# Output blocks of a hybrid encoder held as two 2 KB halves in place of one 4 KB row, right half first

## The chip, the cores and the metric

One NeuronCore of a Trainium2 chip runs the whole program. The metric is the device time of one execution in microseconds (us); where several runs are shown, the median counts. The engines are named as in the profile: PE (TensorE, matrix products), DVE (VectorE), ACT (ScalarE), POOL (GpSimd) and SP, whose queue issues every DMA of this kernel. PEld is the weight load of PE.

## The reference

Two independent inputs, a prompt of 512 positions and a sample of 1024, go through the same encoder layer with shared weights (d = 1024), all in float32.

```
h = RMSNorm(x);  z = h @ w_in
A = windowed attention on q, k, v          # 8 heads, 128-wide window, sinks
B = silu(LayerNorm(dwconv31(a * sigmoid(b))))
x = x + concat(A, B) @ w_out
u = dwconv3(RMSNorm(x) @ w_up)
x = x + (silu(u[:, :2816]) * u[:, 2816:]) @ w_down
return RMSNorm(x)                          # y * rsqrt(mean(y*y) + eps) * norm_final_g
```

The change lies in the last line, the final RMSNorm of the rows, and in the stores of its result: 12 blocks of 128 rows by 1024 columns (8 of the sample, 4 of the prompt).

## The kernel before

The products are made in float32 precision out of three products of a high and a low part (`whi*hi`, `whi*lo`, `wlo*hi`); each high part is an ACT cast, each low part a subtraction on DVE or POOL. The down-projection of the last stage is cut into seven block products (a Strassen-like scheme, `ORDER = (1, 2, 5, 6, 7, 4, 3)`), each over 11 pairs of 128 rows of `w_down` (`p` = 0 to 10). The sums of the products lie in `acc` ("u", "e", "o11", "o12"), to which `with_x` adds the residual.

Product 4 is the last but one. After it the sums `u` and `e` are complete, so six output blocks can be finished while PE works on product 3: `finish` is called for them between the groups of that product, at the steps listed in `done_at`. When product 3 has been made for four further blocks, DVE adds it to `o12` (line 952 of the helper `add`) and `finish` is called for them; for the last two blocks (tt = 2 and 3) the product is made block by block, the left half having been prepared by `left_first`. In this text the output blocks are numbered 1 to 12 in the order of these calls: 1 to 6 within product 3, 7 to 10 after it, 11 and 12 at the end.

`finish` does this for one block, whose halves of 512 columns are called left (n = 0, from `parts[0]`) and right (n = 1): ACT squares each half with an accumulated sum and writes the squares, which nobody reads, into the output buffer `o` (L1471; L1463 for the left half of blocks 11 and 12). POOL turns the two sums into the root factor with three instructions on 128x1 (L1472, L1473, L1474). The left half is scaled by ACT (L1479) and multiplied by `norm_final_g` on POOL (L1480); in blocks 11 and 12 ACT's scaling (L1482) is all, the vector having been multiplied in on DVE before (L1464). The right half is one DVE instruction (L1484). Each half is stored by one DMA of 256 KB on SP (L1485).

Buffers come from `Slots`, a list of 15 buffers "q" of 4096 bytes, 4 "c" of 4224 and 61 "h" of 2048 per partition. `tile` gives out the smallest kind that fits and, in it, the buffer that has been free for longest; a buffer goes back to the end of the list when the program's last reference to it is gone. A new tile in a used buffer waits for all that read or wrote the old one, a store among them. In the last stage the operand halves of product 3 are "h" buffers too: steps p = 4 to 10 are cast while the first blocks are finished, at most four steps (`LEAD`) ahead.

PE and SP run in the order of the program (`manual_schedule`). On ACT, DVE and POOL a planner sorts the instructions when the program is built, and each of these queues is then worked off strictly in that order, so an instruction that waits holds all behind it.

Of the kernel before, what the change touches and what calls it, by code (L numbers as in the profile page):

```python
# [12 lines left out]
AF = mybir.ActivationFunctionType  # L13
ALU = mybir.AluOpType

P = 128
D = 1024
KC = D // P
NT = 512
# [126 lines left out]
def tile_hybrid_encoder(ctx: ExitStack, tc: tile.TileContext, xs, rel_bias, norm_attn_g, w_in,  # L146
                        attn_sink, conv_dw_w, conv_dw_b, conv_ln_g, conv_ln_b, w_out, norm_ffn_g,
                        w_up, ffn_dw_w, ffn_dw_b, w_down, norm_final_g, onehot, outs):
    nc = tc.nc
# [7 lines left out]
    sb = Slots(big, dict(q=(15, 4096), c=(4, 4224), h=(61, 2048), d=(2, 2176), s=(32, 64)), "q", KEEP)  # L157
# [3 lines left out]
    def sm(n):  # L161
        return sb.tile([n])
# [786 lines left out]
    L, R = slice(0, NT), slice(NT, W2)  # L949
# [506 lines left out]
    fins = []  # L1456
    early = {}

    def left_first(tt):

        ss, o = early[tt] = sm(2), sb.tile([D])
        part = cut(o11, tt)
        nc.scalar.activation(o[:, L], part, AF.Square, accum_out=ss[:, 0:1])  # L1463
        nc.vector.tensor_tensor(part, part, fins[0][:, L], op=ALU.mult)  # L1464

    def finish(blk, parts, tail):
        ss, o = early.pop(blk) if tail else (sm(2), sb.tile([D]))
        rs = sm(2)
        for n in range(1 if tail else 0, 2):
            s = slice(n * NT, (n + 1) * NT)  # L1470
            nc.scalar.activation(o[:, s], parts[n], AF.Square, accum_out=ss[:, n:n + 1])  # L1471
        nc.gpsimd.tensor_scalar(rs[:, 0:1], ss[:, 0:1], 1.0 / D, EPS, op0=ALU.mult, op1=ALU.add)  # L1472
        nc.gpsimd.tensor_scalar(rs[:, 1:2], ss[:, 1:2], 1.0 / D, rs[:, 0:1], op0=ALU.mult, op1=ALU.add)  # L1473
        nc.gpsimd.tensor_tensor(rs[:, 1:2], rs[:, 1:2], nhalf[:], op=ALU.pow)  # L1474
        G, b = (GR[1], blk) if blk >= 0 else (GR[0], blk + 4)
        for n in range(2):
            s = slice(n * NT, (n + 1) * NT)
            if n == 0 and not tail:
                nc.scalar.activation(o[:, s], parts[n], AF.Identity, scale=rs[:, 1:2])  # L1479
                nc.gpsimd.tensor_tensor(o[:, s], o[:, s], fins[0][:, s], op=ALU.mult)  # L1480
            elif n == 0:
                nc.scalar.activation(o[:, s], parts[n], AF.Identity, scale=rs[:, 1:2])  # L1482
            else:
                nc.vector.scalar_tensor_tensor(o[:, s], parts[n], rs[:, 1:2], fins[0][:, s], op0=ALU.mult, op1=ALU.mult)  # L1484
            nc.sync.dma_start(G["o"][b * P:(b + 1) * P, s], o[:, s])  # L1485

    made = 0

# [109 lines left out]
    for p, w in [(0, 2), (1, 2), (0, 0), (1, 0)] + [(p, w) for p in range(2, NPAIR) for w in (2, 0)]:  # L1598
        last_group(p, w)
        if w == 0 and p in done_at:  # L1600
            tt = done_at[p]
            finish(4 + tt if tt < 4 else tt - 6, (cut(u, tt), cut(e, tt)), False)
    for tt in (4, 5, 0, 1):
        add(cut(o12, tt), zs[tt // 2][:, (tt % 2) * NT:(tt % 2 + 1) * NT], cut(o12, tt))
        finish(tt if tt < 4 else tt - 8, (cut(o11, tt), cut(o12, tt)), False)
    zs.clear()
    for tt in (2, 3):
        left_first(tt)
        z = wide()
        for p in range(NPAIR):  # L1610
            mm_down(z[:, L], 3, p, tt)
        add(cut(o12, tt), z[:, L], cut(o12, tt))
        finish(tt, (cut(o11, tt), cut(o12, tt)), True)
        del z
# [43 lines left out]
```

## Time and profile before

| | us |
|---|---|
| runs shown | 1562.33, 1561.49, 1563.84 |
| median | 1562.33 |
| span of the profiled execution | 1559.5 |
| median of the runs less that span | 2.8 |
| PE busy in the span | 1505.8 (97%) |
| DVE, ACT, POOL busy | 1126.9, 795.2, 709.7 |
| HBM read, written | 164.74 MB, 62.14 MB |

The span runs from the first to the last event of the profiled execution; the profile gives no other time of that execution, so the 2.8 us are what lies around the span, as far as it can be told. All times within the run below are microseconds from the start of the span. In a row of the timeline stand start, duration, engine, line and operation, then output and inputs by name and the count of instructions merged into the row; in brackets the idle time of that engine just before, and what ended it. A row of the waits reads "engine line waited for: total, times, longest".

### The profile page before, as it was taken

The page shows a single profiled execution, that of the slowest core. Times are in us where ns is not written, and L with a number is a line of the kernel's source. Part 1 is how long each engine was busy: PE and PEld are TensorE (multiplying, and loading weights), DVE is VectorE, ACT ScalarE, POOL GpSimd, SP SyncE. Part 2 cuts the span into 40 slices and gives each one's busy share as a digit, 9 for nine tenths or more (in the row PEclk, how much of TensorE's full clock was granted, in tenths as well). Part 3 has the DMA queues.
Part 4 walks back from the last instruction along what each step waited for, and adds up shares of the span by engine and source line. Part 5 has one row for each costly group of instructions (what it writes and reads, how often), then busy time and mean ns, then how long its engine had stood idle before and what let it go on. Part 6 is the DMA issues. An engine that isn't in the chain of part 4 may idle for free. (4 is left out here: it accounts for less than half of the span.)

```text
span 1559.5 us, 20112 instructions
## 1 busy us (share of the span) xinstructions
PE 1505.8 (97%) x6843; PEld 1228.9 (79%) x6843; DVE 1126.9 (72%) x1604; ACT 795.2 (51%) x1404; POOL 709.7 (46%) x566
## 2 busy tenths in 40 slices
PE   8998998899999999899999999999999999999997
PEld 6787787787888888777777888888888788888885
DVE  7999767858789785334868777777776845569883
ACT  4634654335787786623455445554545543444354
POOL 6652343226666775947434555555544000003355
PEclk9999999899999999999999999999999999999999
DMA  7582334447344346779332333333332582357644
GB/s 229 157 212 78 108 99 124 128 131 226 111 132 130 117 130 182 241 235 305 108 95 75 102 101 102 102 102 102 102 115 75 191 280 82 105 166 233 220 132 162
DMA packets 228780, 227.17 MB, mean 146 GB/s; under 512 B 13268, under 2 KB 168348, under 8 KB 228549
## 3 DMA queue, kind: packets, MB, share of 16 engines
q1 hardware_dynamic: 228677, 225.88, 45.6%
q8 instruction: 54, 0.88, 0.2%
q14 instruction: 49, 0.40, 0.1%
HBM read 164.74 MB, written 62.14 MB: 145 GB/s over the span
## 5 line engine op out<-in xcount | busy, mean ns | idle before, releaser
L193 POOL TENSOR_TENSOR q<-q,q 128x1024 fp32r<-128x1024 f32 x72 | 173.3, 2414 | 93.5 <-ACT q L192 36.7
L955 POOL TENSOR_TENSOR q<-q,q 128x512 fp32r<-128x512 f32 x101 | 140.7, 1398 | 163.8 <-ACT q L1065 151.5
L955 DVE TENSOR_TENSOR h<-h,h 128x512 fp32r<-128x512 f32 (+2 forms) x202 | 158.4, 817 | 66.2 <-ACT h L959 26.1
L1413 PE MATMUL w<-h,h 128*128 128x512 f32 x462 | 181.4, 393 | 0.5 <-DVE q L1200 0.5
L1414 PE MATMUL w<-h,h 128*128 128x512 f32 x462 | 181.5, 393 | 0.0
L1415 PE MATMUL w<-h,h 128*128 128x512 f32 x462 | 181.1, 392 | 0.0
L1079 PE MATMUL w<-h,q 128*128 128x512 f32 x448 | 176.4, 394 | 3.0 <-ACT w L1171 1.6
L1081 PE MATMUL w<-h,q 128*128 128x512 f32 x448 | 175.5, 392 | 1.0 <-POOL q L955 1.0
L1080 PE MATMUL w<-h,q 128*128 128x512 f32 x426 | 166.5, 391 | 0.0
L299 PE MATMUL u<-h,q 128*128 128x512 f32 x400 | 161.1, 403 | 5.0 <-DVE h L852 4.2
L300 PE MATMUL u<-h,q 128*128 128x512 f32 x400 | 158.9, 398 | 0.0
L302 PE MATMUL u<-h,q 128*128 128x512 f32 x384 | 152.2, 396 | 2.7 <-POOL q L193 2.7
L952 POOL TENSOR_TENSOR q<-q,q 128x1024 f32<-128x1024 f32 x12 | 33.1, 2769 | 238.1 <-DMA h<-gb 197.4
L354 DVE SCALAR_TENSOR_TENSOR c<-c,cvw,c 128x512 f32<-128x512 f32 x184 | 137.9, 750 | 2.9
L959 ACT CAST h<-h 128x512 fp32r<-128x512 f32 x120 | 71.8, 619 | 95.9 <-DVE h L955 42.5
L299 PE MATMUL b<-h,q 128*128 128x512 f32 x256 | 102.3, 400 | 2.7 <-DVE d L384 1.9
L1413 PEld LDWEIGHTS w<-h,h 128*128 128x128 f32 x462 | 86.8, 188 | 20.7 <-ACT h L959 0.9
L1415 PEld LDWEIGHTS w<-h,h 128*128 128x128 f32 x462 | 86.7, 188 | 19.7
L852 DVE SCALAR_TENSOR_TENSOR h<-u,fw,h 128x511 f32<-128x511 f32 x88 | 65.4, 744 | 50.8 <-ACT h L856 50.1
L1414 PEld LDWEIGHTS w<-h,h 128*128 128x128 f32 x462 | 86.8, 188 | 19.4
L1079 PEld LDWEIGHTS w<-h,q 128*128 128x128 f32 x448 | 84.2, 188 | 22.5 <-ACT w L1171 2.1
L302 PE MATMUL b<-h,q 128*128 128x512 f32 x256 | 101.3, 396 | 0.0
(417 smaller groups left out, 3680.3 us busy)
## 6 DMA issues: line engine op xcount, KB each, us to landing
q<-in_w_up SPq DMA_DIRECT2D x88, 512.0 KB
ga<-q SPq DMA_DIRECT2D x64, 256.0 KB
h<-ga SPq DMA_DIRECT2D x57, 256.0 KB
q<-in_w_in SPq DMA_DIRECT2D x28, 512.0 KB
h<-in_w_down SPq DMA_DIRECT2D x52, 256.0 KB
q<-in_x_sample SPq DMA_DIRECT2D x15, 512.0 KB
h<-qsd SPq DMA_DIRECT2D x24, 256.0 KB
x1d<-q SPq DMA_DIRECT2D x11, 512.0 KB
```

Source lines behind the costliest of these rows:

```text
L193: (nc.vector if dve else nc.gpsimd).tensor_tensor(lo[:], raw[:], hi[:].bitcast(F32), op=ALU.subtract)
L299: nc.tensor.matmul(out, whi[:, kc, :], hi[:], start=(kc == 0), stop=False)
L300: nc.tensor.matmul(out, whi[:, kc, :], lo[:], start=False, stop=False)
L302: nc.tensor.matmul(out, wlo[:, kc, :], hi[:], start=False, stop=(kc == KC - 1))
L354: nc.vector.scalar_tensor_tensor(acc[:], src(t), w(t), acc[:], op0=ALU.mult, op1=ALU.add)
L955: (eng or nc.vector).tensor_tensor(out, a, b, op=ALU.subtract)
L1079: nc.tensor.matmul(out, whi[:, s], hi[:], start=(start and c == 0), stop=False, **go)
L1080: nc.tensor.matmul(out, whi[:, s], lo[:], start=False, stop=False, **go)
L1081: nc.tensor.matmul(out, wlo[:, s], hi[:], start=False, stop=(stop and c == 3), **go)
L1413: nc.tensor.matmul(out, sh[:, c], th[:], start=(p == 0), stop=False)
L1414: nc.tensor.matmul(out, sh[:, c], tl[:], start=False, stop=False)
L1415: nc.tensor.matmul(out, sl[:, c], th[:], start=False, stop=(p == NPAIR - 1))
```

## The change

An output block is held in two "h" buffers of 2 KB, `o[0]` for the left half and `o[1]` for the right, in place of one "q" buffer of 4 KB. The loop that scales and stores takes the right half first, so its DVE instruction is issued, and its store queued on SP, ahead of the left half's. The number of instructions and of stores stays as it was, and the functions after the change are one line shorter, so that lines 1471 to 1485 become 1470 to 1484.

```diff
     def left_first(tt):
 
-        ss, o = early[tt] = sm(2), sb.tile([D])
+        ss, o = early[tt] = sm(2), [sb.tile([NT]) for _ in range(2)]
         part = cut(o11, tt)
-        nc.scalar.activation(o[:, L], part, AF.Square, accum_out=ss[:, 0:1])
+        nc.scalar.activation(o[0][:], part, AF.Square, accum_out=ss[:, 0:1])
         nc.vector.tensor_tensor(part, part, fins[0][:, L], op=ALU.mult)
 
     def finish(blk, parts, tail):
-        ss, o = early.pop(blk) if tail else (sm(2), sb.tile([D]))
+        ss, o = early.pop(blk) if tail else (sm(2), [sb.tile([NT]) for _ in range(2)])
         rs = sm(2)
         for n in range(1 if tail else 0, 2):
-            s = slice(n * NT, (n + 1) * NT)
-            nc.scalar.activation(o[:, s], parts[n], AF.Square, accum_out=ss[:, n:n + 1])
+            nc.scalar.activation(o[n][:], parts[n], AF.Square, accum_out=ss[:, n:n + 1])
...
-        for n in range(2):
+        for n in (1, 0):
             s = slice(n * NT, (n + 1) * NT)
             if n == 0 and not tail:
-                nc.scalar.activation(o[:, s], parts[n], AF.Identity, scale=rs[:, 1:2])
-                nc.gpsimd.tensor_tensor(o[:, s], o[:, s], fins[0][:, s], op=ALU.mult)
+                nc.scalar.activation(o[n][:], parts[n], AF.Identity, scale=rs[:, 1:2])
+                nc.gpsimd.tensor_tensor(o[n][:], o[n][:], fins[0][:, s], op=ALU.mult)
             elif n == 0:
-                nc.scalar.activation(o[:, s], parts[n], AF.Identity, scale=rs[:, 1:2])
+                nc.scalar.activation(o[n][:], parts[n], AF.Identity, scale=rs[:, 1:2])
             else:
-                nc.vector.scalar_tensor_tensor(o[:, s], parts[n], rs[:, 1:2], fins[0][:, s], op0=ALU.mult, op1=ALU.mult)
-            nc.sync.dma_start(G["o"][b * P:(b + 1) * P, s], o[:, s])
+                nc.vector.scalar_tensor_tensor(o[n][:], parts[n], rs[:, 1:2], fins[0][:, s], op0=ALU.mult, op1=ALU.mult)
+            nc.sync.dma_start(G["o"][b * P:(b + 1) * P, s], o[n][:])
```

The orders below differ from the place of product 3 on; before that nothing moves. A name such as `h20_2215` is buffer 20 of kind h, with a running number of the tile; `s` are sums and factors, `c1` is the vector `norm_final_g`, `w` are PE's banks.

The first place is ACT's queue where blocks 6 to 10 are squared and scaled. Before, all of it lies in three buffers:

```order
L1471 ACTIVATE q5_2201_13880,s12_2200_13879<-q12_1797_11993 128x512
L1471 ACTIVATE q7_2204_13894,s14_2203_13893<-q12_1797_11993 128x512
L1471 ACTIVATE q0_2207_13908,s16_2206_13907<-q2_1794_11963 128x512
L1471 ACTIVATE q5_2201_13880,s12_2200_13879<-q9_1962_12760 128x512
L1471 ACTIVATE q7_2204_13894,s14_2203_13893<-q9_1962_12760 128x512
L1471 ACTIVATE q0_2207_13908,s16_2206_13907<-q8_1959_12728 128x512
L1479 ACTIVATE q5_2201_13880<-q12_1797_11993,s13_2202_13881 128x512
L1479 ACTIVATE q7_2204_13894<-q12_1797_11993,s15_2205_13895 128x512
L1479 ACTIVATE q0_2207_13908<-q2_1794_11963,s17_2208_13909 128x512
L1471 ACTIVATE q5_2210_13922,s18_2209_13921<-q2_1794_11963 128x512
L1471 ACTIVATE q5_2210_13922,s18_2209_13921<-q8_1959_12728 128x512
```

The same place with the change:

```order
L1470 ACTIVATE h50_2204_13860,s10_2202_13858<-q3_1873_12348 128x512
L1470 ACTIVATE h39_2207_13886,s12_2206_13885<-q12_1797_11993 128x512
L1478 ACTIVATE h26_2203_13859<-q13_1716_11610,s11_2205_13861 128x512
L1470 ACTIVATE h50_2211_13901,s14_2210_13900<-q12_1797_11993 128x512
L1470 ACTIVATE h20_2208_13887,s12_2206_13885<-q9_1962_12760 128x512
L1470 ACTIVATE h26_2212_13902,s14_2210_13900<-q9_1962_12760 128x512
L1478 ACTIVATE h39_2207_13886<-q12_1797_11993,s13_2209_13888 128x512
L1478 ACTIVATE h50_2211_13901<-q12_1797_11993,s15_2213_13903 128x512
L1470 ACTIVATE h20_2215_13916,s16_2214_13915<-q2_1794_11963 128x512
L1470 ACTIVATE h39_2216_13917,s16_2214_13915<-q8_1959_12728 128x512
L1470 ACTIVATE h26_2219_13931,s18_2218_13930<-q2_1794_11963 128x512
L1470 ACTIVATE h50_2220_13932,s18_2218_13930<-q8_1959_12728 128x512
```

Before, blocks 7, 8 and 9 (tiles 2201, 2204, 2207) take turns in q5, q7, q0 and block 10 (2210) is back in q5, the buffer of block 7. Now blocks 8 (2211 and 2212) and 10 (2219 and 2220) share h26 and h50 with block 6, and blocks 7 and 9 share h20 and h39: a block's halves lie where the halves of the block two before lay, the left where the right one lay.

The second place is ACT's queue where blocks 1 to 3 are scaled and the last operands of product 3 are cast. Before:

```order
L959 CAST h12_2172_13710<-h42_2121_13465 128x512
L1471 ACTIVATE q7_2170_13698,s2_2169_13697<-q11_1875_12365 128x512
L959 CAST h27_2185_13767<-h26_2133_13526 128x512
L1471 ACTIVATE q5_2157_13641,s0_2156_13640<-q1_1719_11629 128x512
L1471 ACTIVATE q5_2157_13641,s0_2156_13640<-q11_1875_12365 128x512
L1471 ACTIVATE q7_2170_13698,s2_2169_13697<-q1_1719_11629 128x512
L959 CAST h42_2187_13771<-h20_2140_13546 128x512
L1479 ACTIVATE q0_2179_13735<-q6_1713_11592,s5_2180_13736 128x512
L1479 ACTIVATE q5_2157_13641<-q1_1719_11629,s1_2158_13642 128x512
L1479 ACTIVATE q7_2170_13698<-q1_1719_11629,s3_2171_13699 128x512
```

With the change:

```order
L1478 ACTIVATE h55_2181_13737<-q6_1713_11592,s5_2183_13739 128x512
L1478 ACTIVATE h46_2157_13641<-q1_1719_11629,s1_2159_13643 128x512
L1478 ACTIVATE h35_2171_13699<-q1_1719_11629,s3_2173_13701 128x512
L1470 ACTIVATE h26_2196_13796,s6_2194_13794<-q10_1872_12334 128x512
L1397 CAST h46_2178_13720<-h9_2123_13481 128x512
L959 CAST h17_2186_13754<-h50_2129_13506 128x512
L959 CAST h9_2190_13774<-h20_2140_13546 128x512
L1470 ACTIVATE h50_2195_13795,s6_2194_13794<-q6_1713_11592 128x512
L1397 CAST h55_2192_13778<-h39_2145_13563 128x256
```

Four casts of steps p = 8, 9 and 10 now stand behind the scaling of blocks 1 to 3, and three of them write into buffers (h46, h17, h55) from which halves of those blocks are stored.

The third place is the end of DVE's queue: the sums of the last two blocks (L952, from banks w0 and w1), the multiplication of their left halves (L1464) and the scaling of right halves. Before:

```order
L952 TENSOR_TENSOR q4_1960_12743<-w0_65_13938,q4_1960_12743 128x512
L1464 TENSOR_TENSOR q14_1795_11977<-q14_1795_11977,c1_2078_13288 128x512
L1484 SCALAR_TENSOR_TENSOR q5_2210_13922<-q8_1959_12728,s19_2211_13923,c1_2078_13288 128x512
L1484 SCALAR_TENSOR_TENSOR q7_2213_13935<-q4_1960_12743,s21_2214_13973,c1_2078_13288 128x512
L1464 TENSOR_TENSOR q14_1795_11977<-q14_1795_11977,c1_2078_13288 128x512
L952 TENSOR_TENSOR q4_1960_12743<-w1_66_13986,q4_1960_12743 128x512
L1484 SCALAR_TENSOR_TENSOR q0_2216_13983<-q4_1960_12743,s26_2217_14021,c1_2078_13288 128x512
```

With the change:

```order
L952 TENSOR_TENSOR q4_1960_12743<-w0_65_13949,q4_1960_12743 128x512
L1483 SCALAR_TENSOR_TENSOR h50_2220_13932<-q8_1959_12728,s19_2221_13933,c1_2078_13288 128x512
L1464 TENSOR_TENSOR q14_1795_11977<-q14_1795_11977,c1_2078_13288 128x512 x2
L1483 SCALAR_TENSOR_TENSOR h20_2224_13946<-q4_1960_12743,s21_2225_13984,c1_2078_13288 128x512
L952 TENSOR_TENSOR q4_1960_12743<-w1_66_13998,q4_1960_12743 128x512
L1483 SCALAR_TENSOR_TENSOR h26_2228_13995<-q4_1960_12743,s26_2229_14033,c1_2078_13288 128x512
```

The right half of block 10 (2220) and both left halves now come ahead of the scaling of block 11 (2224); the last sum (from w1) still stands behind that scaling.

## The prediction

> **What bounds the kernel now.** I read the engines' busy time first, then busy time by stretches of the end, then the timeline of the engines there. The page says that PE bounds the run as a whole:
>
> ```profile
> PE 1505.8 (97%) x6843; PEld 1228.9 (79%) x6843; DVE 1126.9 (72%) x1604; ACT 795.2 (51%) x1404; POOL 709.7 (46%) x566
> ```
>
> The stretches (start:end, length, then busy time of PE, PEld, DVE, ACT, POOL, granted clock, DMA share, GB/s) show where that ends:
>
> ```profile
> 1530.00:1540.00 10.00, 10.00 (x45) 8.16 (x44) 4.12 (x7) 5.46 (x15) 5.23 (x11) 1.00 0.36 134
> 1540.00:1550.00 10.00, 7.89 (x34) 6.04 (x33) 4.28 (x5) 5.14 (x13) 7.67 (x11) 1.00 0.43 158
> 1550.00:1560.00 10.00, 0.00 (x0) 0.00 (x0) 3.70 (x4) 2.17 (x4) 2.85 (x5) 0.64 0.42 157
> ```
>
> PE is full up to 1547.89, and the last 11.6 us of the 1559.5 us span are without it. The orders show the program unchanged up to product 3, where PE has no gap, so all that can be won lies in those 11.6 us. DVE's timeline there, after PE's last product:
>
> ```profile
> 1547.27 0.40 PE L1414 MATMUL w<-h,h 128*128 128x512 f32 x1
> 1547.50 0.39 PE L1415 MATMUL w<-h,h 128*128 128x512 f32 x1
> ...
> 1548.19 0.69 DVE L1464 TENSOR_TENSOR q<-q,c 128x512 f32<-128x512 f32 x1 [4.82 <-ACT q L1463]
> 1548.80 0.74 DVE L1484 SCALAR_TENSOR_TENSOR q<-q,s,c 128x512 f32<-128x512 f32 x1
> 1550.34 1.74 DVE L1484 SCALAR_TENSOR_TENSOR q<-q,s,c 128x512 f32<-128x512 f32 x1 [0.80 <-POOL s L1474]
> 1552.01 0.68 DVE L1464 TENSOR_TENSOR q<-q,c 128x512 f32<-128x512 f32 x1
> 1552.61 0.68 DVE L952 TENSOR_TENSOR q<-w,q 128x512 f32<-128x512 f32 x1
> 1555.14 0.75 DVE L1484 SCALAR_TENSOR_TENSOR q<-q,s,c 128x512 f32<-128x512 f32 x1 [1.85 <-POOL s L1474]
> ```
>
> The last sum (L952) could start at about 1547.95 and starts at 1552.61, since four older instructions stand ahead of it on DVE, the first of them waiting 4.82 us. What follows the sum (square, root, scaling, store) takes 1559.5 - 1552.61 = 6.9 us. So at most 4.65 us can be won. Who made DVE late is on ACT:
>
> ```profile
> 1522.97 0.63 ACT L1471 ACTIVATE q<-q 128x512 f32<-128x512 f32 x1 [5.07 <-DMA out_prompt<-q]
> 1523.60 0.62 ACT L1471 ACTIVATE q<-q 128x512 f32<-128x512 f32 x1
> ...
> 1533.51 0.63 ACT L1471 ACTIVATE q<-q 128x512 f32<-128x512 f32 x1 [0.96 <-DMA out_sample<-q]
> ...
> 1536.14 0.63 ACT L1471 ACTIVATE q<-q 128x512 f32<-128x512 f32 x1 [1.90 <-DMA out_sample<-q]
> ...
> 1545.03 0.63 ACT L1471 ACTIVATE q<-q 128x512 f32<-128x512 f32 x1 [3.32 <-DMA out_prompt<-q]
> ...
> 1547.43 0.63 ACT L1463 ACTIVATE q<-q 128x512 f32<-128x512 f32 x1 [1.06 <-POOL s L1474]
> ```
>
> Squares wait for stores: three buffers serve all output blocks, block n waits for both stores of block n-3, and one late square holds the ACT queue for all. The last row names POOL, which was long done; by the buffers it is block 11 waiting for the right half's store of block 8. From issue to the square that it frees (the first row merges the two stores of block 1, the second is the later one of them):
>
> ```profile
> 1520.15 0.81 SPq L1485 DMA_DIRECT2D out_prompt<-q  x2
> ...
> 1520.58 0.38 SPq L1485 DMA_DIRECT2D out_prompt<-q  x1
> ...
> 1542.69 0.36 SPq L1485 DMA_DIRECT2D out_prompt<-q  x1
> ...
> 1544.69 0.33 SPq L1485 DMA_DIRECT2D out_prompt<-q  x1
> ```
>
> That is 1522.97 - 1520.58 = 2.39 us, 2.34 us to 1545.03 and 2.74 us to 1547.43; I take 2.39.
>
> **The change part by part.** Counts of instructions and stores stay: 24 stores of 256 KB, the same squares and scalings. A 2 KB tile has the same 512 columns per instruction, so durations stay too. What moves is who waits. After the last operand is cast, four "h" buffers are free, and two pairs serve blocks 4 to 12. Block n then waits for stores of block n-2 instead of n-3 (a loss), but each half waits for one half's store alone, and blocks 1 to 3, which have buffers of their own, start earlier (gains). So the end is again a chain of stores and squares. I follow it with POOL's and DVE's rows:
>
> ```profile
> 1507.73 1.20 POOL L1473 TENSOR_SCALAR s<-s,s 128x1 f32<-128x1 f32 x1
> 1508.90 2.85 POOL L952 TENSOR_TENSOR q<-q,q 128x1024 f32<-128x1024 f32 x1
> 1511.71 1.00 POOL L1474 TENSOR_TENSOR s<-s,nhalf 128x1 f32<-128x1 f32 x1
> ...
> 1517.12 4.25 POOL L1480 TENSOR_TENSOR q<-q,c 128x512 f32<-128x512 f32 x3
> ...
> 1523.78 0.19 POOL L1472 TENSOR_SCALAR s<-s 128x1 f32<-128x1 f32 x1 [2.41 <-ACT q L1471]
> 1524.48 0.26 POOL L1473 TENSOR_SCALAR s<-s,s 128x1 f32<-128x1 f32 x1 [0.51 <-ACT q L1471]
> 1524.83 0.55 POOL L1474 TENSOR_TENSOR s<-s,nhalf 128x1 f32<-128x1 f32 x1
> 1525.41 0.75 DVE L1484 SCALAR_TENSOR_TENSOR q<-q,s,c 128x512 f32<-128x512 f32 x1 [6.45 <-POOL s L1474]
> ...
> 1532.02 1.29 POOL L1480 TENSOR_TENSOR q<-q,c 128x512 f32<-128x512 f32 x1 [0.83 <-ACT q L1479]
> ...
> 1538.61 0.71 ACT L1479 ACTIVATE q<-q,s 128x512 f32<-128x512 f32 x1
> ```
>
> From the start of a right square to POOL's second sum is 1524.48 - 1523.60 = 0.88 us; from there to the first scaling 1525.41 - 1524.48 = 0.93 us; together 1.81. A multiplication takes 1.29 us alone and 1.42 us in a series of three.
>
> - Start. Two residual adds (L952) run on POOL, with the 1.20 us sum of an early block between them; that sum goes behind. The second add ends at 1511.75 now, so at 1510.5 after the change, or near 1509 if the first add, too, starts earlier (its own sum on DVE stands behind one low part fewer). I take 1510.0.
> - Blocks 1 to 3 on POOL: before, from 1511.71 to 1517.12 + 4.25 = 1521.37, 9.7 us for all but two of their instructions. At undisturbed durations the three blocks need 3 x (0.28 + 0.35 + 0.52) + 3 x 1.29 = 7.3 us (0.28 and 0.52 are the distances to the next instruction as estimated from 0.19 and 0.55 us). I take 8.7: end 1518.7. SP issues a store every 0.43 us (1520.15 to 1520.58), so the left half of block 3 is issued at 1519.6.
> - The last cast (p = 10) waits for that store: 1522.0. Behind it on ACT stand the two squares of block 5; the right one starts at 1522.0 + 0.31 + 0.62 = 1522.9. Root at 1524.7; POOL multiplies block 4 until 1526.0, and its left half is stored.
> - Block 6, right: 1526.0 + 2.39 = 1528.4, root 1530.2, ACT's scaling 0.71, POOL 1.29: stored at 1532.2.
> - Block 8, right: 1534.6. PE's sums for blocks 7 to 10 are due from 1531.9, so the store ends last. Root 1536.4; POOL multiplies blocks 7 and 8: 1539.25.
> - Block 10, right: 1541.65, root 1543.45; block 9 multiplied and stored at 1544.9.
> - Block 11, right: 1547.3, root 1549.1, its scaling on DVE holds the last sum by 0.65: the sum starts at 1549.75, where 1552.61 was. The second of the two L1464 ahead waits for the left square of block 12, and that for block 10's right store at about 1545.3: square at 1547.9, L1464 over at about 1549.3, so it may cost 0.2 us more, which the allowance below takes in.
>
> So the sum is 1549.75 - 1552.61 = -2.9 us. The chain has POOL's 128x1 instructions at their short durations, and beside DVE they can be longer:
>
> ```profile
> 1548.24 0.68 POOL L1472 TENSOR_SCALAR s<-s 128x1 f32<-128x1 f32 x1 [0.81 <-ACT q L1463]
> 1549.02 0.65 POOL L1473 TENSOR_SCALAR s<-s,s 128x1 f32<-128x1 f32 x1
> ```
>
> Against 0.19 and 0.26 us that is 0.88 us for one block; I allow 0.4 in all. The forecast is -2.5 us: span 1557.0, and with the 2.8 us around it, as in the runs shown, 1562.33 - 2.5 = **1559.8 us**.
>
> The three casts that write into stored halves cost nothing as long as PE is not there yet. Counting back from its end, step p = 8 begins 102 products of 0.23 us (1547.27 to 1547.50) before 1547.6, at 1524.1; p = 10 at 1529.7. The casts follow the stores of blocks 1 to 3, the last at 1522.0, so p = 8 has about 3.5 us to spare, p = 10 about 7. The store of the right half first costs nothing at the very end: before, both halves of block 12 are ready at the same time, and its two stores follow each other in either order.
>
> One row speaks against the change. A right scaling that starts just behind a POOL multiplication takes longer:
>
> ```profile
> 1540.92 4.25 POOL L1480 TENSOR_TENSOR q<-q,c 128x512 f32<-128x512 f32 x3
> 1540.99 1.78 DVE L1484 SCALAR_TENSOR_TENSOR q<-q,s,c 128x512 f32<-128x512 f32 x1 [0.44 <-POOL s L1474]
> ```
>
> 1.78 us against 0.75, so 1.03 us lost, and the right half's store now stands ahead of the left one's on SP. In the chain the multiplication is the longer way (a series of two ends 2.84 us after its start, the hindered scaling 1.85), so I cost it at nothing; it returns in the slow rival. The Trainium skill, page "SBUF — State Buffer", section "Who interferes with whom", says that a DVE instruction with two SBUF inputs and a GpSimd instruction that reads SBUF share a read interface, and that whichever issues first keeps it for its whole length. The trace agrees that one waits, though for 1.03 us and not the whole 1.42; by the rule the scaling would end some 0.3 us later, still within the 2.84, and the sum would stay.
>
> **The rivals.** *The chain runs without disturbance and PE's end decides.* If the adds end at 1509 and blocks 1 to 3 take 7.3 us, all is 2.4 us earlier, the sum waits for PE at 1547.95, and the gain is the whole 4.65: 1557.7 us. It comes out faster by over 0.2% (3.1 us) as soon as the chain is 0.25 us shorter than the undisturbed sum. For it: DVE idles at the start, where it delayed POOL before. Against it: a hold anywhere on the chain is passed on, since no slack is left between the turns. Chance 0.40.
>
> *Two pairs of buffers are too few.* From block 4's store to the last sum are four turns, 1526.0 to 1549.75, of 5.9 us each. If in each turn a scaling on DVE gets in first and POOL waits for it (0.75) and its two sums are stretched as above (0.88), a turn is 1.63 longer, the sum starts 6.5 us later, at 1556.3, and the time is 1562.33 + 3.7 = 1566.0 us. It is slower by 3.1 us from 1.5 us a turn on. For it: the rows of 1.78, 0.68 and 0.65 us. Against it: before, such holds took single places, not each turn. Chance 0.11.
>
> *PE waits for an operand behind a store.* If the stores of blocks 1 to 3 land over 3.5 us late, PE stops at p = 8; to cost 3.1 us in the end PE would have to finish at 1555.7, 7.8 us late, so the stores over 11 us: about 1565.5 us and more. Chance 0.03. That the change does not do what it says is no case: the order of ACT shows the "h" buffers.
>
> **How the numbers follow.** Differences within 0.2%, 3.1 us, are about what a measurement of this kernel can tell from no change; the three runs spread over 2.35 us. My likeliest case, a gain of 2.5 us, lies inside that, and has 0.46 with the chains up to no gain or a small loss. Faster has 0.40, slower 0.11 + 0.03 = 0.14. The range reaches down to the PE-bound case with 0.2 us for the runs' spread, 1557.5, and up to 1564.0, a loss of 1.7 us (four turns each 1.15 us longer than summed); 0.18 is left out, the slower cases and the upper end of the middle one.
>
> **What would show it.** Right: the last L952 starts near 1549.8, PE ends at 1547.9 as before, the squares of block 8, 10 and 11 wait for DMA, and block 1's first store is issued near 1513 instead of 1520.15. The prediction is wrong if PE has a gap between 1524 and 1532, if the last sum starts right at PE's end, or if a turn from store to store lasts over 7 us.

## The result and the profile after

The kernel got slightly slower: the median of 22 runs is 1565.93 us (1564.01 to 1573.48), against 1563.20 us (1561.38 to 1567.74) for 22 runs of the kernel before; the ratio is 1.0021, with a 95% interval of 1.0011 to 1.003. A second comparison gave 1.0009 (0.9994 to 1.0025), which by itself can't be told from no change. The forecast was 2.5 us faster, and 1565.93 us lies outside its range (up to 1564.0 us).

The profiled execution took 1566.91 us with a span of 1565.1 us; 1.8 us lie around the span, not the 2.8 us that the prediction took. Its span is no measure of the change: PE began product 3, up to which the program is the same, at 1505.19, 3.22 us later than in the profile before (1501.97). In the ten later profiles that place came 0.1 to 11.2 us later. So I measure from PE's end, which follows the start of product 3 by 45.7 to 46.1 us in all profiles but one (blocks 4 and 5 elsewhere, below). I call **tail** what lies between the end of PE's last product and the end of the span. Before it was 1559.5 - 1547.89 = 11.6 us.

The last full stretch of busy times, the changed kernel (columns as in the prediction; in the stretches from 1500 to 1550 PE is full):

```profile
1550.00:1560.00 10.00, 1.28 (x6) 0.71 (x4) 6.73 (x7) 5.65 (x14) 6.28 (x11) 0.73 0.37 139
```

PE's last product and DVE's timeline behind it, the changed kernel:

```profile
1550.89 0.40 PE L1415 MATMUL w<-h,h 128*128 128x512 f32 x1
...
1552.12 1.75 DVE L1483 SCALAR_TENSOR_TENSOR h<-q,s,c 128x512 f32<-128x512 f32 x1 [0.70 <-POOL s L1473]
1553.79 1.75 DVE L1464 TENSOR_TENSOR q<-q,c 128x512 f32<-128x512 f32 x1
1556.89 0.69 DVE L1464 TENSOR_TENSOR q<-q,c 128x512 f32<-128x512 f32 x1 [1.35 <-ACT h L1463]
1557.50 0.75 DVE L1483 SCALAR_TENSOR_TENSOR h<-q,s,c 128x512 f32<-128x512 f32 x1
1558.16 0.69 DVE L952 TENSOR_TENSOR q<-w,q 128x512 f32<-128x512 f32 x1
```

PE ends at 1551.29, and the tail is 1565.1 - 1551.29 = 13.8 us, 2.2 more than before. The last sum (L952) starts 6.9 us behind PE's end; before it was 4.7. What follows the sum takes 6.9 us in both. So DVE is later still, and again ACT shows why, by squares that wait for stores of the block two before:

```profile
1536.07 0.63 ACT L1470 ACTIVATE h<-q 128x512 f32<-128x512 f32 x1 [1.61 <-DMA out_sample<-h]
...
1543.13 0.63 ACT L1470 ACTIVATE h<-q 128x512 f32<-128x512 f32 x1 [1.03 <-DMA out_sample<-h]
...
1550.29 0.63 ACT L1470 ACTIVATE h<-q 128x512 f32<-128x512 f32 x1 [0.23 <-DMA out_prompt<-h]
...
1555.50 0.63 ACT L1470 ACTIVATE h<-q 128x512 f32<-128x512 f32 x1 [1.84 <-DMA out_sample<-h]
```

These are the right squares of blocks 6, 8, 10 and 11. The first three wait for the left halves of blocks 4, 6 and 8, whose stores SP issued here:

```profile
1533.96 0.33 SPq L1484 DMA_DIRECT2D out_sample<-h  x1
1540.12 0.33 SPq L1484 DMA_DIRECT2D out_sample<-h  x1
1547.86 0.33 SPq L1484 DMA_DIRECT2D out_prompt<-h  x1
```

The chain is the predicted one. From block 4's store to the last sum it lasts 1558.16 - 1533.96 = 24.2 us, where 1549.75 - 1526.0 = 23.75 were predicted. It begins too late. ACT, DVE and POOL where it begins, the changed kernel:

```profile
1507.58 3.50 DVE L955 TENSOR_TENSOR h<-h,h 128x512 fp32r<-128x512 f32 x2
1507.74 2.79 POOL L952 TENSOR_TENSOR q<-q,q 128x1024 f32<-128x1024 f32 x1 [12.68 <-DVE q L952]
1511.00 1.21 DVE L952 TENSOR_TENSOR q<-w,q 128x1024 f32<-128x1024 f32 x1
...
1512.29 2.79 POOL L952 TENSOR_TENSOR q<-q,q 128x1024 f32<-128x1024 f32 x1 [1.76 <-DVE q L952]
...
1521.68 3.00 POOL L1479 TENSOR_TENSOR h<-h,c 128x512 f32<-128x512 f32 x2
1521.74 1.77 DVE L1483 SCALAR_TENSOR_TENSOR h<-q,s,c 128x512 f32<-128x512 f32 x1 [1.70 <-POOL s L1473]
1523.44 2.51 DVE L955 TENSOR_TENSOR h<-h,h 128x512 fp32r<-128x512 f32 x2
1525.98 0.64 ACT L1470 ACTIVATE h<-q 128x512 f32<-128x512 f32 x1 [3.51 <-DVE h L955]
1527.25 2.07 DVE L955 TENSOR_TENSOR h<-h,h 128x512 fp32r<-128x512 f32 x3 [1.30 <-DMA out_sample<-h]
1529.39 0.19 POOL L1471 TENSOR_SCALAR s<-s 128x1 f32<-128x1 f32 x1 [4.71 <-ACT h L1470]
```

Three things lie here. The second residual add on POOL ends at 1515.08, 36.2 us ahead of PE's end, no earlier than before (36.1): its own sum on DVE still waits for two L955, which take 1.75 us each beside POOL's first add. Block 4's right square goes into a buffer whose last reader is a low part of an operand (L955), and that subtraction is queued on DVE behind the right scalings of blocks 1 to 3, the last of which waits for POOL's root: the square starts at 1525.98 after 3.51 us. Behind it on ACT and DVE stand casts and low parts that write into stored halves and wait for the stores, and between them the other squares of blocks 4 and 5. POOL, through which the chain goes, is idle for 4.71 us.

### The profile page after: what moved, and what is told of

The parts are those of the page before. It is cut to its first block, busy times and chain, and to the rows that moved or that the text cites. A ratio compares the mean times of both kernels' runs of the same rounds, so it can differ in the third digit from the quotient of the medians.

```text
span 1565.1 us, 20101 instructions
## 1 busy us (share of the span) xinstructions
PE 1506.1 (96%) x6843; PEld 1228.4 (78%) x6843; DVE 1129.8 (72%) x1604; ACT 797.7 (51%) x1404; POOL 708.3 (45%) x566
## 5 line engine op out<-in xcount | busy, mean ns | idle before, releaser
L955 POOL TENSOR_TENSOR q<-q,q 128x512 fp32r<-128x512 f32 x101 | 140.1, 1392 | 163.8 <-ACT q L1065 151.5
L955 DVE TENSOR_TENSOR h<-h,h 128x512 fp32r<-128x512 f32 (+2 forms) x202 | 158.8, 818 | 69.3 <-ACT h L959 25.7
L952 POOL TENSOR_TENSOR q<-q,q 128x1024 f32<-128x1024 f32 x12 | 33.1, 2770 | 253.4 <-DVE q L952 236.9
```

What stands on the lines that cost most here:

```text
L955: (eng or nc.vector).tensor_tensor(out, a, b, op=ALU.subtract)
```

## The experiments

Two causes were open: the late start (theory S) and a rotation only two blocks deep (theory D); before them, whether it was the order (R1) or the cutting in itself (R2). Ratios are to the kernel before, run on the same chip; places and tails are of one profile each. The diffs are shortened: `...` stands for lines left out, and a row that begins with a bracket or a call is the changed part of a line that stands in `left_first` and in `finish`. The planner sorts the queues anew for each kernel, so an edit of the buffers also moves other instructions.

**The kernel before, again.**

> The kernel before once more, for its profile: all theories expect the tail of its first profile to repeat, 11.6 us (11.0 to 12.2), with the last sum on DVE 4.7 us behind PE's end. If it lies at 9.8 or less, the gain seen with the right half first alone is only scatter of the profiles.

The last sum starts 4.9 us behind PE's end (1557.27 and 1552.35), the tail is 1564.2 - 1552.35 = 11.8 us; the first profile had 4.7 and 11.6. So the 9.8 us of the order alone, below, are more than the scatter of this kernel's two profiles.

**The changed kernel, again.**

> The changed kernel once more, to see how far a tail (from the end of PE's last product to the end of the span) and a start repeat. Theory S (the chain starts late: the squares of blocks 1 to 5 wait on ACT behind subtractions and casts that share the h buffers) and theory D (two pairs make every turn too long) both expect what the first profile shows: the last sum on DVE about 6.9 us behind PE's end, tail 13.8 (13.0 to 14.6), ratio 1.001 to 1.003. Rival N (the tail varies by 2 us or more from one execution to the next, whatever the kernel): tail under 12.5 or over 15.

The last sum came 7.2 us behind PE's end (1557.46 and 1550.22), tail 14.2 us, ratio 1.0009 (0.9994 to 1.0025). The tail repeats within 0.4 us, so rival N falls; the ratio alone would not have shown the loss.

**The order alone.**

```diff
-        for n in range(2):
+        for n in (1, 0):
```

> The kernel before with one edit: the right half is scaled and stored first; a block stays one 4 KB row. The measure is the tail, from PE's last product to the end of the span: 11.6 us before, 13.8 after. Theory T (the two pairs of h buffers, and the operands that share them, make the tail longer): nothing of that is here, so the tail stays at 11.6 (11.0 to 12.2) and the ratio at 1.000 (0.999 to 1.001). Rival R1 (the right half first makes it, since DVE's scaling then starts just behind a POOL multiplication and both stretch): the tail is near 13.8 and the ratio near 1.002.

DVE's last sum and PE's last product:

```profile
1555.02 0.68 DVE L952 TENSOR_TENSOR q<-w,q 128x512 f32<-128x512 f32 x1
...
1551.81 0.39 PE L1415 MATMUL w<-h,h 128*128 128x512 f32 x1
```

The sum is 2.8 us behind PE's end, tail 1562.0 - 1552.2 = 9.8 us, ratio 0.999 (0.9974 to 1.0006). R1 falls. Theory T missed too: it expected no change, and the tail is 1.8 to 2 us shorter. In time that is within the interval.

**The halves alone**, left first:

```diff
 # the changed kernel
-        for n in (1, 0):
+        for n in range(2):
```

> The changed kernel with the left half first again: two 2 KB halves from the h buffers, old order. Theory T: the late start and the two pairs are all here, so the tail is 13 to 14.5 us and the ratio to the kernel before 1.002 (1.001 to 1.003). Rival R1 (the order makes it): the tail is back at 11.6 and the ratio at 1.000.

```profile
1557.11 0.68 DVE L952 TENSOR_TENSOR q<-w,q 128x512 f32<-128x512 f32 x1
...
1547.39 0.40 PE L1415 MATMUL w<-h,h 128*128 128x512 f32 x1
```

The last sum (first row) is 9.3 us behind PE's end, tail 1565.1 - 1547.79 = 17.3 us, ratio 1.0037 (1.0024 to 1.005). The sign is T's, the size larger than it expected: among the two pairs the right half first is worth 3.1 to 3.5 us of tail, about 1 of them behind the last sum (8.0 us in place of 6.9). So the two parts of the change work against each other, and the halves in "h" buffers are the part that costs.

**Three pairs that nothing shares.**

```diff
-[sb.tile([NT]) for _ in range(2)]
+[sb.tile([NT], among=k) for k in "qc"]
```

> The changed kernel, right half first, but its halves do not lie in h buffers: left halves take turns in three q buffers, right halves in three c buffers. So the rotation is three blocks deep again, each half waits for one half's store alone, and no operand of product 3 is cast into a stored half. Theory T: the tail is at most 11.6 us (10.0 to 11.6) and the ratio 0.998 to 1.000. Rival R2 (cutting the row into halves, or the right half first, is bad in itself, whatever the buffers): tail near 13.8, ratio near 1.002.

The last sum is 3.1 us behind PE's end (1562.21 and 1559.09), tail 1569.2 - 1559.09 = 10.1 us, ratio 0.9993 (0.9976 to 1.0009). Theory T has both numbers. Cutting rows into halves is not bad in itself; R2 falls. Depth and sharing changed together here; the next two take them apart.

**Only the start.** Blocks 1 to 3 elsewhere, blocks 4 to 12 in the same two "h" pairs. On ACT the squares of blocks 4 and 5 come in another order (4 left, 5 right, 4 right, 5 left, where the changed kernel has 4 right, 4 left, 5 left, 5 right); from the scaling of block 4 on the order is the same:

```diff
...
+    def halves():
+        count[0] += 1
+        return [sb.tile([NT], among=k) for k in ("qc" if count[0] <= 3 else "hh")]
...
-[sb.tile([NT]) for _ in range(2)]
+halves()
```

> The changed kernel, but the halves of blocks 1 to 3 lie in q and c buffers; blocks 4 to 12 take the same two pairs of h buffers in the same order as in the changed kernel. So only the start differs: the squares of blocks 1 to 3 wait for no subtraction that reads an operand, and no operand is cast into a stored half. Theory S: block 4's left half is stored 3 us or more earlier than in the changed kernel (counted from PE's end), four turns of 6.0 us follow, and the last sum comes 2 to 4 us behind PE's end; tail 9 to 11 us, ratio 0.998 to 1.000. Theory D: the last sum stays 6 us or more behind PE's end, tail 13 to 14.5, ratio 1.001 to 1.003.

SP's stores of the left halves of blocks 4, 6 and 8:

```profile
1532.06 0.51 SPq L1490 DMA_DIRECT2D out_sample<-h  x1
1539.02 0.33 SPq L1490 DMA_DIRECT2D out_sample<-h  x1
1546.28 0.33 SPq L1490 DMA_DIRECT2D out_prompt<-h  x1
```

DVE's last sum and PE's last product:

```profile
1556.65 0.68 DVE L952 TENSOR_TENSOR q<-w,q 128x512 f32<-128x512 f32 x1
...
1553.80 0.39 PE L1415 MATMUL w<-h,h 128*128 128x512 f32 x1
```

The last sum is 2.5 us behind PE's end (1554.19), tail 9.4 us, ratio 0.9984 (0.9968 to 1.0001). From block 4's store to the sum it is 24.6 us, as long as in the changed kernel, but that store comes 22.1 us ahead of PE's end in place of 17.3. Theory S holds: with the start undone nothing of the loss is left, in the tail or in the time (median 1560.74 us, where the changed kernel had 1565.52 on the same chip).

**Only the depth.** All twelve blocks in two pairs of "q" and "c" buffers (a third pair is held back until block 12):

```diff
...
+        if not held:
+            held.append([sb.tile([NT], among=k) for k in "qc"])
...
+        return [sb.tile([NT], among=k) for k in "qc"]
```

> The changed kernel, but all twelve blocks take turns in just two pairs of halves, lefts in two q and rights in two c buffers, and no operand shares them. Against the run with three such pairs only the depth differs (two blocks in place of three). Theory S: from block 3 on five turns of about 6 us, which begin as soon as blocks 1 and 2 are stored; the last sum 2 to 5 us behind PE's end, tail 9 to 12, ratio 0.998 to 1.001. Theory D: the turns stretch to 7 us and more, the last sum 7 us or more behind PE's end, tail 14 or more, ratio 1.002 or more.

Two stores of left halves (blocks 2 and 4) with a square and POOL's multiplications between them, then the last sum and PE's last product:

```profile
1528.55 0.33 SPq L1496 DMA_DIRECT2D out_prompt<-q  x1
...
1530.63 0.63 ACT L1482 ACTIVATE q<-q 128x512 f32<-128x512 f32 x1
...
1533.05 2.99 POOL L1491 TENSOR_TENSOR q<-q,c 128x512 f32<-128x512 f32 x2
...
1536.07 0.33 SPq L1496 DMA_DIRECT2D out_sample<-q  x1
...
1565.15 0.68 DVE L952 TENSOR_TENSOR q<-w,q 128x512 f32<-128x512 f32 x1
...
1554.11 0.39 PE L1415 MATMUL w<-h,h 128*128 128x512 f32 x1
```

The turn from block 2's store to block 4's lasts 7.5 us: 2.1 to the square, 2.4 to the multiplications, 3.0 for two of them. The sum is 10.6 us behind PE's end (1554.50), tail 17.6 us, ratio 1.0018 (1.0002 to 1.0035). Here theory S missed and D has its numbers (the ratio, expected at 1.002 or more, all but): two blocks deep instead of three costs 17.6 - 10.1 = 7.5 us of tail when the chain runs through all twelve blocks. That does not make the depth the cause in the changed kernel: its turns did not stretch as a whole (24.2 us where 23.75 were predicted), and with the start undone two pairs from block 4 on had a tail of 9.4 us, no longer than that of three pairs, 10.1.

**Blocks 4 and 5 elsewhere**, blocks 1 to 3 in shared "h" buffers again:

```diff
 # the kernel of "Only the start"
-("qc" if count[0] <= 3 else "hh")
+("qc" if count[0] in (4, 5) else "hh")
```

> The changed kernel, but the halves of blocks 4 and 5 lie in q and c buffers; blocks 1 to 3 stay in h buffers into which operands are cast and subtracted later, and blocks 6 to 12 take the two pairs of h buffers. Theory S (the first block that takes the shared pairs is late, since its squares wait for subtractions on DVE that stand behind the right scalings of blocks 1 to 3; the turns behind it are as priced): the first such block is now block 6, whose right square stays as late as block 4's was, some 25 us ahead of PE's end; but two blocks fewer follow, so the last sum comes 1 to 3 us behind PE's end, tail 8 to 10, ratio 0.997 to 0.999. Rival (what is late are the stores of blocks 1 to 3 themselves, and with them the operands and PE): the last sum stays 5 us or more behind PE's end or PE has a gap, tail 12 or more, ratio 1.000 or more.

PE's timeline at step p = 8:

```profile
1529.50 0.39 PE L1415 MATMUL w<-h,h 128*128 128x512 f32 x1
1532.75 0.50 PE L1413 MATMUL w<-h,h 128*128 128x512 f32 x1 [2.86 <-ACT h L1397]
...
1533.92 0.79 PE L1415 MATMUL w<-h,h 128*128 128x512 f32 x1 [0.42 <-DVE h L955]
1534.51 0.63 PE L1413 MATMUL w<-h,h 128*128 128x512 f32 x1
1534.93 0.63 PE L1414 MATMUL w<-h,h 128*128 128x512 f32 x1
```

The last sum is 1.9 us behind PE's end (1560.43 and 1558.53), tail 8.9 us, the numbers of theory S, but they do not bear it out. PE stops for a cast into block 1's stored half and its low part, and ends 5.0 us later than the same products would: of the rival's signs, the gap came. The tail looks short because PE's end is late. Counted from the start of product 3 (1507.63) the last sum comes after 52.8 us, as late as in the changed kernel (53.0), where the run with only the start undone has 48.4. Whether theory S would hold without the stop, this run can't say: block 6's right square lies 28.0 us ahead of PE's end, 23.0 without the stop, where 25 were expected. The ratio, 0.9999 (0.9981 to 1.0017), shows neither gain nor loss. The stop is the prediction's third rival. In the changed kernel it is one step away; PEld's timeline there has idle times of 0.24 and 0.43 us that end with the same cast and low part:

```profile
1527.27 0.19 PEld L1413 LDWEIGHTS w<-h,h 128*128 128x128 f32 x1 [0.24 <-ACT h L1397]
1528.00 0.19 PEld L1415 LDWEIGHTS w<-h,h 128*128 128x128 f32 x1 [0.43 <-DVE h L955]
```

**Six whole rows**, left first, and then the same with DVE for the left halves of blocks 7 to 10 (`ended` holds the blocks finished so far):

```diff
+    kinds = deque("qcqcqcqcqcqc")
...
-sb.tile([D])
+sb.tile([D], among=turn_of())
...
 # second kernel
-            if n == 0 and not tail:
+            if n == 0 and not tail and len(ended) < 6:
...
-            elif n == 0:
+            elif n == 0 and tail:
```

> The kernel before, whole 4 KB rows, left half first, but the rows take turns among three q and three c buffers, six blocks deep. Theory T (in both kernels the tail is a chain of stores and squares through too few buffers): no square waits for a store any more, the last sum on DVE starts right behind PE's last product, and the tail is 7 to 8.5 us, the ratio 0.997 to 0.998. Rival R3 (the tail is set by how fast POOL and DVE finish twelve blocks, not by buffers): the tail stays at 10.5 us or more, the ratio at 0.9995 or more.

Last sum 3.9 us behind PE's end (1554.71 and 1550.79), tail 10.8 us, ratio 0.9989 (0.9975 to 1.0004): the tail is rival R3's, the ratio lies between the two. Block 10's scaling waits 3.18 us for its root, behind POOL's multiplications:

```profile
1550.90 0.75 DVE L1489 SCALAR_TENSOR_TENSOR c<-q,s,c 128x512 f32<-128x512 f32 x1 [3.18 <-POOL s L1479]
1551.57 0.68 DVE L952 TENSOR_TENSOR q<-w,q 128x512 f32<-128x512 f32 x1
1554.04 0.75 DVE L1489 SCALAR_TENSOR_TENSOR q<-q,s,c 128x512 f32<-128x512 f32 x1 [1.79 <-POOL s L1479]
1554.71 0.68 DVE L952 TENSOR_TENSOR q<-w,q 128x512 f32<-128x512 f32 x1
```

But R3's "not by buffers" is not shown, since the buffers are still in the way. The squares of blocks 7 to 12 now wait, one behind the other, for stores of the block six before; the left squares of blocks 11 and 12 (L1468 here) are held by that, and through the multiplications of the same halves (L1469) they hold DVE:

```profile
1538.31 0.63 ACT L1468 ACTIVATE q<-q 128x512 f32<-128x512 f32 x1 [0.71 <-DMA out_sample<-q]
...
1539.06 0.69 DVE L1469 TENSOR_TENSOR q<-q,c 128x512 f32<-128x512 f32 x1 [11.52 <-ACT q L1468]
```

DVE's sums of blocks 7 to 10 stand behind these and begin at 1540.99, though PE was done with those blocks' products by 1535.5. So POOL's series starts late as well; what it costs without this wait is open.

> The kernel with six whole 4 KB rows in turn, left half first, and for blocks 7 to 10 both halves are scaled on DVE in one instruction each, so that ACT's scaling and POOL's multiplication of these four are gone. With six rows the last sum was 3.9 us behind PE's end, since block 10's scaling on DVE waited for its root behind POOL's multiplications. Theory P (behind the buffers POOL's series of multiplications is next): the last sum comes within 1.5 us of PE's end, tail 7 to 9 us, ratio 0.996 to 0.998. Rival Q (DVE, with four more scalings ahead of the sum, is as late): last sum 3 us or more behind PE's end, tail 10 or more, ratio 0.9985 or more.

```profile
1552.26 0.68 DVE L952 TENSOR_TENSOR q<-w,q 128x512 f32<-128x512 f32 x1
...
1550.80 0.39 PE L1415 MATMUL w<-h,h 128*128 128x512 f32 x1
```

The last sum (first row) is 1.1 us behind PE's end, tail 1559.1 - 1551.19 = 7.9 us; median 1560.30 against 1564.55 us, ratio 0.9969 (0.9955 to 0.9984). Theory P has its numbers, and this version beats both kernels (the changed one had 1565.52 us on the same chip).

## Why the prediction was wrong

All places in us from PE's end (minus: ahead of it); the prediction's axis is that of the profile before, PE's end 1547.89:

| step | predicted | changed kernel | only the start undone |
|---|---|---|---|
| second residual add over | -37.9 | -36.2 | -36.6 |
| POOL done with blocks 1 to 3 | -29.2 | -26.6 | (other order) |
| block 5's right square | -25.0 | -21.2 | -31.3 |
| block 4's left half stored | -21.9 | -17.3 | -22.1 |
| block 6's left half stored | -15.7 | -11.2 | -15.2 |
| block 8's left half stored | -8.6 | -3.4 | -7.9 |
| last sum starts | 1.9 | 6.9 | 2.5 |

- **The step that failed is the start**, from "I take 1510.0" to "block 4 multiplied until 1526.0". Measured, block 4's store is 4.6 us late: 1.7 from the second add, 0.9 from POOL's blocks 1 to 3, 1.2 to block 5's square, 0.8 to the store. The prediction counted one wait of the shared buffers there, the last cast behind a store. It did not count that the squares go into buffers which subtractions on DVE still read, nor that low parts are written into stored halves too. Blocks 1 to 3 elsewhere gave back 4.8 us at that store and 4.4 us at the last sum, though the second add was as late there (-36.6). So the shared buffers of blocks 1 to 3 carry nearly all of the loss, and the late add costs nothing that shows. Not taken apart was how much of it is squares behind subtractions, how much operands behind stores, and how much the new order that the planner made of it: the squares of blocks 4 and 5 then came ahead of POOL's multiplications of blocks 1 and 2, and POOL did not idle for them.
- **The turns were right in sum**: 23.75 us predicted from block 4's store to the last sum, 24.2 measured, 24.6 with the start undone. One by one they were 6.2, 7.7 and, for the last two together, 10.3 us, where 6.2, 7.05 and 10.5 were predicted. A turn over 7 us, which the prediction named as a sign that it is wrong, was no such sign: its own second turn is that long. From store to the square that it frees it was 2.1, 3.0 and 2.4 us (1536.07, 1543.13 and 1550.29 less the stores above) for 2.39. With the start undone the last sum, at 2.5, lies where the prediction with its allowance of 0.4 has it, at 2.3. In part that is luck, since block 4's store got to its place there by another order on POOL than the one summed.
- **The bound was right**: behind PE's end at most 4.65 us could be won, and no run won more; the last version has 3.7 of them.
- **The right half first** was costed at nothing in the chain. It shortens the tail, by about 1.9 us in the old rows and 3.3 among the two pairs, though the hindered scalings of 1.75 us are there.
- **The rivals.** "Two pairs are too few" gave 1566.0 us, almost the measured time, by a way that was not taken: four turns of 7.57 us did not come, only the second was that long, and together they lasted 24.2 us. "PE waits for an operand" had 3.5 us to spare at p = 8; in the changed kernel nothing was left, and PE lost 0.2 us by its end (3.39 behind the profile before, 3.22 at the start of product 3; nothing in the second profile of it). "PE's end decides" had its chance from a chain that starts early, and fell with the start.

## What to carry to other kernels

Output buffers taken from a pool that operands still use are not free when the list says so: for each new tile list its buffer's last readers and its next writer, find where those stand in the strict queues, and follow that through before pricing the steady turns. A chain can be sized right from its first turn on and still come out wrong by its first link. When runs scatter by more than the change is worth, measure from an event up to which the programs are the same, here the start of product 3; PE's end serves as well only while the edit does not make PE wait.

## What the hardware showed unexpectedly

- In the run with blocks 4 and 5 elsewhere 3.25 us passed from the start of one of PE's products to the next (1529.50 to 1532.75), 2.86 of them idle, and PE then ran at half its pace: products 0.42 us apart in place of 0.23, until 1536.6. The stretches there (columns as in the prediction, PE's granted clock third from the end):

```profile
1533.00:1535.00 2.00, 1.58 (x5) 0.93 (x5) 1.97 (x3) 1.31 (x3) 0.32 (x1) 0.58 1.03 384
1535.00:1537.00 2.00, 2.00 (x7) 1.57 (x6) 0.77 (x3) 1.37 (x6) 1.30 (x4) 0.57 1.01 379
1537.00:1539.00 2.00, 2.00 (x10) 1.61 (x9) 0.64 (x1) 0.61 (x1) 1.92 (x2) 1.00 0.40 153
```

The granted clock is 0.58 and 0.57 and back at 1.00 from 1537, so a stop costs more than its length: 5.0 us for 3.3 of waiting (2.86 and 0.42). The Trainium skill, page "TensorE: Matmul & The Clock Gate", section "Part 1: The HAM clock gate (the "warmup" mystery)", says that an idle window of about 3.4 us halves PE's clock and some 3.4 us of work restore it. The trace agrees in the pace and in the length of the slow stretch; the gap here was a little shorter than that window.

- Two low parts beside POOL's residual add took 3.50 us together, where one alone just before took 0.69 us (1505.84), so 2.1 us more. The Trainium skill, page "SBUF — State Buffer", section "Who interferes with whom", says that DVE instructions with two SBUF inputs contend with GpSimd's reads; this row agrees.
